# A one-core encoder layer: the places of TensorE's two operands modulo 512 bytes are changed by pads

## The chip, the core and the metric

The kernel runs on one core of one Trainium2 chip. The metric is the device time of one execution in microseconds (us). The kernel before took 1360.14 us, the median of three runs (1357.89 to 1361.29). About 0.3% of that, 4.1 us, is what a measurement of this kernel can tell from no change.

## What is computed

The program is one layer (depth 1) of a hybrid encoder, in fp32, for a prompt of 1,024 rows and a sample of 64 rows that continues a cache of 512. The reference, cut to its core:

```python
z = einsum('btd,de->bte', x, w_in)               # one projection, split into q, k, v of FoX, gate, SGU u and v, q, k, v of stick-breaking
o_f = softmax(q_f k_f / 8 + c_t - c_s) v_f       # 6 heads x 64, causal, c = cumsum(log_sigmoid gate)
o_s = stick_breaking(q_s k_s / 8) v_s            # 6 heads x 64, strictly causal
o_g = gelu(u) * (tril(w_s) layer_norm(gelu(v)) + b_s)
mix = (per_head_rms_norm([o_f, o_g, o_s]) * g_mix) @ w_out
x1  = layer_norm(2**0.25 * x + mix)
y   = layer_norm(2**0.25 * x1 + square(relu(x1 @ w_up)) @ w_down)
```

The outputs are y and the new rows of k, v, the log gate and the normalised v.

## The kernel before, in words

**Operands.** Every fp32 operand of a large product is kept as a high and a low part (type fp32r), and a product is three passes: high x high, high x low, low x high. So each product is a train of matmuls that accumulate into one PSUM bank, and each matmul has its own weight load (PEld), which runs while the matmul ahead of it streams. The operand that is loaded is called stationary here (128 columns), the one that streams is called moving (256, 262, 288 or 512 columns).

**Stages, in order of time.** From 0 to about 530 us: projections of keys and values (`tok_mm`, L490, moving `wkvfox`, `wkvsb`, `wu`, `wv`, stationary the transposed input `xT`), projections of queries (L631, moving `xT`, stationary `wqfox`, `wqsb`), and attention: scores (L691), transposes by the identity (L739), products with the values (L749 to L752), the sample's products (L829 to L875). To about 660 us: the output projection `mix` (L373, moving `w_out`, stationary `oTb`). To about 980 us: the up projection (`product`, L1441; stationary `ws`, `wa`, moving `xo`). It works by seven products a block pair over two row groups, `NS = (288, 256)`, so that twelve matmuls of 288 columns and twelve of 256 mostly alternate. To the end: the down projection (`Down.product`, L1906, and the sample's L1950 and L1952; moving `wd`, stationary `h4a`, `h4b`), then the last norm.

The lines of the matmuls say which operand is which, since the call's second argument is stationary and its third is moving:

```python
490   nc.tensor.matmul(acc[0:n, c0:c0 + n1 - n0], xT[k // 4][:, k % 4, c:c + n], wt[:, k, hw, n0:n1],
373   nc.tensor.matmul(acc[0:m], oT[:, k, hx, 0:m], wo[k // 4][hw][:, k % 4, cs],
631   nc.tensor.matmul(acc[:, 0:w], wq[:, k, hw, :], xT[k // 4][:, k % 4, c:c + w],
749   nc.tensor.matmul(o[:, 0:256], v0, pth[:, 0, 0:256], start=(m == 0), stop=False)
1441  nc.tensor.matmul(z, w[:, hw, k], xop(s, bo, hx)[:, k, :], start=(new and k == 0 and j == 0),
1906  nc.tensor.matmul(z, h[:, hx, q, o], wset[self.c % 2][q][:, hw, wb],
```

**Order.** Four tables written out in the kernel (`ORDER`, one for TensorE, ScalarE, VectorE and GpSimd) fix the order of each engine's instructions. They are the same before and after. DMAs go out on SyncE's queue in program order.

**Where tiles lie.** Tiles come from pools. `cp`, `big` (tag `xw`: `xT`, `xo`, and `wd` later) and `sp` grow from the left end of a partition, `sa`, `lp` and `dp` serve the attention and the two MLP halves. A tile's address follows from the tiles that its pool placed earlier, so a small unused tile moves what comes behind it. `pad(pool, n)` (L242) places such a tile of n bytes a partition.

**Place.** In this document the place of a matmul is the start of its moving operand minus the start of its stationary operand, in bytes within a partition, modulo 512. It follows from the addresses that the built program gives its tiles. Both programs have 8,827 matmuls in the same order, as many as the trace has matmul records, so each record has its place. Place 448 means that the moving operand starts 64 bytes below the stationary one.

Of the kernel before, what the change touches and what calls it, by code (L numbers as in the profile page):

```python
# [13 lines left out]
F32 = mybir.dt.float32  # L14
F32R = mybir.dt.float32r
# [6 lines left out]
P = 128  # L22
PASSES = ((0, 0), (0, 1), (1, 0))
D = 1024
# [4 lines left out]
NB = TP // P  # L29
NT = NB + 1  # L30
# [13 lines left out]
ROWS = 7  # L44
# [129 lines left out]
def _build(nc, tc, a, es):  # L174
    def trows(t):
        return P if t < NB else TS

    cp = es.enter_context(tc.tile_pool(name="cp", bufs=1, side="left"))
    big = es.enter_context(tc.tile_pool(name="big", bufs=2, side="left"))
# [9 lines left out]
    def flat(n):  # L189
        return a[n].rearrange("l b t h d -> (l b t) (h d)")  # L190
# [7 lines left out]
    ident = cp.tile([P, P], F32, name="ident")  # L198
# [15 lines left out]
    def lo_sub(eng, out, src, hi):  # L214
        eng.tensor_tensor(out, src, hi.bitcast(F32), op=ALU.subtract)  # L215
# [26 lines left out]
    def pad(pool, n):  # L242

        n_pad.append(pool.tile([P, n // 4], F32, name=f"pad{len(n_pad)}", tag=f"pad{len(n_pad)}"))
# [161 lines left out]
    ps = es.enter_context(tc.tile_pool(name="ps", bufs=2, space=PSUM))  # L406
    p12 = ExitStack()
    sp = p12.enter_context(tc.tile_pool(name="sp", bufs=1, side="left"))
    lsum = sp.tile([P, NT, 6], F32, name="lsum")
    nc.gpsimd.memset(lsum, 1.0)  # L410
    gmx = sp.tile([P, KT], F32, name="gmx")
    with ExitStack() as p1:
        sa = p1.enter_context(tc.tile_pool(name="sa", bufs=1, side="right"))
# [4 lines left out]
        def mask(name, base, fill):  # L418
            m = sp.tile([P, P], F32, name=name + "_f", tag="gl", bufs=3)
            nc.gpsimd.memset(m, 0.0)  # L420
            nc.gpsimd.affine_select(m, m, pattern=[[-1, P]], compare_op=ALU.is_ge,
                                    fill=fill, base=base, channel_multiplier=1)
            r = sp.tile([P, P], F32R, name=name)
            nc.vector.tensor_copy(r, m)
            return r

        m_fox = mask("m_fox", 0, BIG)
        m_sb = mask("m_sb", -1, -BIG)

        xT = [big.tile([P, 4, 2 * TT], F32R, name=f"xT{i}", tag="xw") for i in range(2)]  # L430

# [8 lines left out]
        def x_trans(t, xr):  # L440
            n = trows(t)
            for g in range(2):
                pt = ps.tile([P, 4, P], F32, name=f"xtp{t}_{g}", tag=("s", "pt")[g], bufs=2)
                for k in range(4):
                    c = (4 * g + k) * P
                    nc.tensor.transpose(pt[:, k, 0:n], xr[0:n, c:c + P], ident[0:n, 0:n])
                hi = xT[g][:, :, t * P:t * P + n]
                nc.scalar.activation(hi, pt[:, :, 0:n], AF.Copy)
                lc = LO + t * P if t < NB else TT
                lo_sub(nc.vector, xT[g][:, :, lc:lc + n], pt[:, :, 0:n], hi)  # L450
# [30 lines left out]
        def tok_mm(acc, c0, wt, t, n0, n1, ks=range(KT)):  # L481
            seq = []
            for k in ks:
                if t < NB:
                    seq += [(P, k, hx * LO + t * P, hw) for (hx, hw) in PASSES]
                else:
                    two = [(P, k, TP, 0), (TS, k, TP, 1)]
                    seq += two if k == ks[0] else two[::-1]
            for i, (n, k, c, hw) in enumerate(seq):
                nc.tensor.matmul(acc[0:n, c0:c0 + n1 - n0], xT[k // 4][:, k % 4, c:c + n], wt[:, k, hw, n0:n1],  # L490
                                 start=(i == 0), stop=(i == len(seq) - 1))
                if (i + 1) % 8 == 0 and i + 1 < len(seq):
                    yield 0.109 * 8
                    flush()

        def fold(eng, out, acc, c0, n):
            eng.tensor_tensor(out, out, acc[TS:P, c0:c0 + n], op=ALU.add)
# [76 lines left out]
        def k_stack(pk, kpiece, n, nm):  # L574
            for h in range(2):
                nc.scalar.activation(kpiece[0:DH, h, 0:n], pk[h * DH:(h + 1) * DH, 0:n], AF.Copy)
                lo_sub(nc.vector, kpiece[DH:P, h, 0:n], pk[h * DH:(h + 1) * DH, 0:n], kpiece[0:DH, h, 0:n])

        def kv_stage(st, tiles, kpiece, vpiece):
            j, wkv, nv = st["nm"], st["wkv"], st["nv"]  # L580
            kcol = st["hp"] * P
            kvs = []
            for i, t in enumerate(tiles):
                n = trows(t)
                if st["first"]:
                    x_trans(t, xrs[t])
                acc = ps.tile([P, 512], F32, name=f"kv{j}_{t}", tag="acc", bufs=2)
                yield from tok_mm(acc, 0, wkv, t, 0, nv)
                kv = sa.tile([P, 256], F32, name=f"kvs{j}_{t}", tag="kvs", bufs=2)
                kvs.append(kv)  # L590
                nc.scalar.activation(kv[0:n], acc[0:n, 0:256], AF.Copy)
                if nv > 256:
                    nc.vector.tensor_copy(fx[0:n, t, :], acc[0:n, 256:262])
                if t == NB:
                    fold(nc.vector, kv[0:n], acc, 0, 256)
                    if nv > 256:
                        fold(nc.vector, fx[0:n, t, :], acc, 256, 6)
                g = 0 if t < NB else 1
                r0 = t * P if t < NB else 0
                nc.sync.dma_start(flat(st["ok"][g])[r0:r0 + n, kcol:kcol + P], kv[0:n, 0:P])  # L600
                nc.sync.dma_start(flat(st["ov"][g])[r0:r0 + n, kcol:kcol + P], kv[0:n, P:2 * P])
                vs = kv[0:n, P:2 * P].rearrange("p (h c) -> p h c", h=2)
                vh = vpiece[0:n, i, :, 0:DH]
                nc.gpsimd.tensor_copy(vh, vs)
                lo_sub(nc.gpsimd, vpiece[0:n, i, :, DH:P], vs, vh)
                if i + 1 < len(tiles):
                    yield 0.109 * 8

            def finish():
                tot = 0  # L610
                pk = ps.tile([P, 2 * P], F32, name=f"pk{j}_{tiles[0]}", tag="tr", bufs=1)
                for kv, t in zip(kvs, tiles):
                    n = trows(t)
                    nc.tensor.transpose(pk[:, tot:tot + n], kv[0:n, 0:P], ident[0:n, 0:n])
                    tot += n
                k_stack(pk[:, 0:tot], kpiece, tot, f"{j}_{tiles[0]}")

            later.append(finish)
            yield 0.109 * 8
# [387 lines left out]
        for fox, hp in ((True, 2), (True, 1), (True, 0), (False, 0), (False, 1), (False, 2)):  # L1007
            first = not pairs
# [34 lines left out]
        def kv_all(j, us=range(5)):  # L1043
            st = pairs[j]
            nm = st["nm"]
            for u in us:
                if u == 4:
                    if st["first"]:
                        forget(0)
                    yield from slots("kn", 1, 1)  # L1050
                    st["kn"] = sa.tile([P, 2, TS], F32R, name=f"kn{nm}", tag="kn", bufs=1)
                    st["vn"] = sa.tile([P, 1, 2, P], F32R, name=f"vn{nm}", tag="vn", bufs=1)
                    yield from kv_stage(st, [NB], st["kn"], st["vn"])
                    continue
                yield from slots("kp", 1, 8)
                kt = sa.tile([P, 2, 256], F32R, name=f"kp{nm}_{u}", tag="kp", bufs=10)
                if st["first"] and u == 0:
                    pad(sa, 64)
                vt = sa.tile([P, 2, 2, P], F32R, name=f"vp{nm}_{u}", tag="vp", bufs=10)
                st["kp"].append(kt)  # L1060
                st["vp"].append(vt)
                yield from kv_stage(st, [2 * u, 2 * u + 1], kt, vt)
# [3 lines left out]
        def slots(tag, n, cap):  # L1066
            while live[tag] + n > cap:
                yield None
            live[tag] += n
# [225 lines left out]
    xo1 = []  # L1295
# [197 lines left out]
    for i in range(MIXED, NT):  # L1493
        t = ORD[i]
# [13 lines left out]
            back.append(x_samp())  # L1508

    n1 = 4 * 2 * NS[1]  # L1510
    xw = [big.tile([P, 16 + q * n1], F32R, name=f"xo1{q}", tag="xw")[:, 16:] for q in (4, 3)]
    xo1 += [x.rearrange("p (o k h c) -> p o k h c", o=q, k=4, h=2) for x, q in zip(xw, (4, 3))]
    prep0_b(raws0, 1 - ORD.index(ORD[-1]) % 2)
    x2, x3 = x_pair(2), x_pair(3)
# [112 lines left out]
    with p3:  # L1627
# [55 lines left out]
        t = ORD[-1]  # L1683
# [52 lines left out]
        with in_order(border):  # L1736
            ch = chain(1, 0)
            ch.product(0)
            raw = up_load(2)
# [114 lines left out]
    with ExitStack() as p3:  # L1854
        dp = p3.enter_context(tc.tile_pool(name="dp", bufs=1, side="right", reuse_waits="tile"))
# [102 lines left out]
        lst = {}  # L1958

        def norm(t):  # L1960
            if t not in lst:

                lst[t] = ident[:, 16 * t:16 * t + 16] if t < NB else dp.tile([P, 40], F32, name="lstb")
            return lst[t]

        def moments(t, half, n=P):
# [295 lines left out]
    for eng, e in (("PE", nc.tensor), ("ACT", nc.scalar), ("DVE", nc.vector), ("POOL", nc.gpsimd)):  # L2262
        left = [i for i in traced[from_here:] if i.engine == e.engine]
        prev = None
        for word in ORDER[eng].split():
            n, k = (int(x or d) for x, d in zip(re.match(r"(\d*)\+?(\d*)", word).groups(), (1, 0)))
# [30 lines left out]
```

## Time and profile before

| | |
|---|---|
| median of three runs | 1360.14 us |
| the profiled execution's own time | 1360.14 us |
| span of its trace | 1358.4 us |
| mean granted TensorE clock | 0.992 |
| PE (matmul) busy, share of the span | 1305.0 us, 96% |
| PEld (weight load) | 1190.8 us, 88% |
| DVE, ACT, POOL | 73%, 53%, 46% |
| chain that ended last, by engine | PE 71%, DVE 12%, DMA 6%, POOL 4%, ACT 4%, issue 3% |

[...] The pace is the time between the starts of two matmuls, and where a row of the chain of waits holds a train of n matmuls of one kind, its length divided by n is the pace.

### The profile page before, as it was taken

How to read it: one execution, taken by the hardware profiler on the slowest of the kernel's cores; microseconds unless marked ns; L12 is line 12 of the kernel's file. 1: busy time of each engine (PE TensorE's matmuls, PEld its weight loads, DVE VectorE, ACT ScalarE, POOL GpSimd, SP SyncE). 2: the span in 40 equal slices, each digit the busy share in tenths (PEclk: the TensorE clock that was granted, in tenths of full speed). 3: DMA queues.
4: the chain of work that ended last, by engine and by line, in shares of the span. 5: the costliest groups of instructions: out<-in, count | busy, mean ns of one | idle time of the engine just before them, and what ended most of it. 6: DMA issues, size and time to landing. Idle time of an engine off the chain costs nothing.

```text
span 1358.4 us, 24318 instructions
## 1 busy us (share of the span) xinstructions
PE 1305.0 (96%) x8827; PEld 1190.8 (88%) x8827; DVE 998.3 (73%) x1797; ACT 719.3 (53%) x1561; POOL 620.6 (46%) x666
## 2 busy tenths in 40 slices
PE   7999999999988998999999999999999999999996
PEld 7998989999988998778899999999987787887874
DVE  4577666676889289779886777778688677768777
ACT  4366666576656376335523222233267676767765
POOL 3222222255775356766512221212176665665647
PEclk9999999999999999999999999999999999999998
DMA  7435565131312257532234444344568334434333
GB/s 228 111 113 152 150 203 150 52 97 40 91 31 69 65 164 262 155 122 76 79 123 142 156 137 155 122 160 144 180 242 282 124 132 159 138 126 161 121 118 132
DMA packets 158048, 185.64 MB, mean 137 GB/s; under 512 B 27740, under 2 KB 116124, under 8 KB 157928
## 3 DMA queue, kind: packets, MB, share of 16 engines
q1 hardware_dynamic: 155832, 183.01, 42.1%
q8 instruction: 70, 1.15, 0.4%
q10 hardware_dynamic: 2096, 1.07, 0.3%
q14 instruction: 50, 0.41, 0.1%
HBM read 117.65 MB, written 60.10 MB: 131 GB/s over the span
## 4 chain that ended last, share of the span: by engine, by line
PE 71%; DVE 12%; DMA 6%; POOL 4%; ACT 4%; issue 3%; SPq 1%; ACTq 0%; DVEq 0%; POOLq 0%
PE A L1906 10%; PE zA L1441 9%; PE mx L373 6%; PE zD L1441 6%; PE D L1906 5%; PE kvsb L490 5%; PE kvfox L490 3%; PE zB L1441 3%; PE zC L1441 3%; PE B L1906 2%; DMA rwo<-w_out 2%; PE qsb L631 2%; PE Sfox L691 1%; PE qfox L631 1%; DVE snsb L675 1%
## 5 line engine op out<-in xcount | busy, mean ns | idle before, releaser
L215 POOL TENSOR_TENSOR wa<-wr,wa 128x512 fp32r<-128x512 f32 x41 | 62.3, 1546 | 217.9 <-ACT wa L1379 217.9
L215 POOL TENSOR_TENSOR wd<-rd,wd 128x512 fp32r<-128x512 f32 x77 | 101.1, 1324 | 104.2 <-ACT wd L1379 71.4
L373 PE MATMUL mx<-xT,oTb 128*128 128x512 f32 (+1 forms) x416 | 104.0, 401 | 1.8 <-DVE oTb L215 1.3
L1441 PE MATMUL zD<-xo,ws 128*128 128x288 f32 (+1 forms) x720 | 95.9, 287 | 0.2 <-DVE hh L1455 0.2
L1441 PE MATMUL zA<-xo,ws 128*128 128x288 f32 (+1 forms) x720 | 95.7, 287 | 0.0
L373 PEld LDWEIGHTS mx<-xT,oTb 128*128 128x128 f32 (+1 forms) x416 | 75.7, 187 | 20.3 <-DVE oTb L215 2.2
L1441 PEld LDWEIGHTS zD<-xo,ws 128*128 128x128 f32 x720 | 92.2, 188 | 0.5 <-DVE hh L1455 0.5
L490 PE MATMUL kvfox<-wkvfox,xT 128*128 128x256 f32 (+3 forms) x624 | 89.3, 291 | 3.1 <-ACT wkvfox L466 3.0
L1441 PEld LDWEIGHTS zA<-xo,ws 128*128 128x128 f32 x720 | 92.2, 188 | 0.0
L1573 POOL TENSOR_TENSOR rd<-rd 128x512 f32<-128x512 f32 x56 | 79.5, 1420 | 25.9 <-DVE b L215 23.6
L490 PE MATMUL kvsb<-wkvsb,xT 128*128 128x256 f32 (+1 forms) x624 | 88.0, 285 | 0.3 <-ACT wkvsb L466 0.3
L677 POOL TENSOR_TENSOR sgsb<-sgsb,snsb 128x127 f32<-128x127 f32 (+7 forms) x48 | 59.5, 1243 | 57.5 <-DVE snsb L675 50.4
L1379 ACT ACTIVATE wd<-rd 128x512 fp32r<-128x512 f32 x105 | 63.6, 624 | 40.5 <-POOL rd L1573 23.0
L490 PEld LDWEIGHTS kvfox<-wkvfox,xT 128*128 128x128 f32 (+1 forms) x624 | 80.6, 191 | 4.5 <-ACT wkvfox L466 3.4
L1906 PE MATMUL A<-wd,wd 128*128 128x512 f32 x312 | 83.1, 395 | 1.3 <-DVE acc L1873 1.0
L675 DVE TENSOR_TENSOR_SCAN snsb<-snsb,one 128x128 f32<-128x128 f32 (+7 forms) x48 | 72.2, 1508 | 10.7 <-ACT snsb L674 9.3
L490 PEld LDWEIGHTS kvsb<-wkvsb,xT 128*128 128x128 f32 (+1 forms) x624 | 79.0, 186 | 0.7 <-ACT wkvsb L466 0.5
L1906 PEld LDWEIGHTS A<-wd,wd 128*128 128x128 f32 x312 | 58.2, 188 | 16.7 <-DVE acc L1873 2.2
L1452 ACT ACTIVATE sn<-zA 128x256 f32<-128x256 f32 (+1 forms) x80 | 30.9, 389 | 74.4 <-PE zA L1441 65.7
L1906 PE MATMUL A<-wd,h4a 128*128 128x512 f32 x240 | 64.3, 394 | 1.1 <-DVE acc L1873 0.7
L1662 ACT ACTIVATE ws<-wr 128x1024 fp32r<-128x1024 f32 x28 | 29.1, 1055 | 62.3 <-DVE wr L1391 62.3
L1873 DVE TENSOR_TENSOR acc<-acc,A 128x512 f32<-128x512 f32 x73 | 49.1, 679 | 10.9 <-PE A L1906 10.9
(551 smaller groups left out, 3738.6 us busy)
## 6 DMA issues: line engine op xcount, KB each, us to landing
h_dr<-hh SPq DMA_DIRECT2D x30, 512.0 KB, 3.2
rd<-w_down SPq DMA_DIRECT2D x30, 512.0 KB, 4.4
wr<-w_up SPq DMA_DIRECT2D x13, 1024.0 KB, 5.5
hr<-h_dr SPq DMA_DIRECT2D x31, 384.0 KB, 4.3
h_dr<-hh SPq DMA_DIRECT2D x30, 384.0 KB, 3.7
raw<-w_in SPq DMA_DIRECT2D x44, 256.0 KB, 3.3
wo_dr<-swo SPq DMA_DIRECT2D x32, 256.0 KB, 2.2
xT<-wo_dr SPq DMA_DIRECT2D x8, 1024.0 KB, 8.1
```

The costliest lines, as they stand in the source:

```text
L215: eng.tensor_tensor(out, src, hi.bitcast(F32), op=ALU.subtract)
L373: nc.tensor.matmul(acc[0:m], oT[:, k, hx, 0:m], wo[k // 4][hw][:, k % 4, cs], start=(i == 0), stop=(i == len(seq) - 1))
L490: nc.tensor.matmul(acc[0:n, c0:c0 + n1 - n0], xT[k // 4][:, k % 4, c:c + n], wt[:, k, hw, n0:n1], start=(i == 0), stop=(i == len(seq) - 1))
L631: nc.tensor.matmul(acc[:, 0:w], wq[:, k, hw, :], xT[k // 4][:, k % 4, c:c + w], start=(i == 0), stop=(i == len(seq) - 1))
L675: nc.vector.tensor_tensor_scan(g[:, 0:n][:, ::-1], g[:, 0:n][:, ::-1], one.broadcast_to([P, n]), 1.0, op0=ALU.mult, op1=ALU.bypass)
L677: nc.gpsimd.tensor_tensor(s[:, 0:n - 1], s[:, 0:n - 1], g[:, 1:n], op=ALU.mult)
L1379: nc.scalar.activation(hi, raw, AF.Copy)
L1441: nc.tensor.matmul(z, w[:, hw, k], xop(s, bo, hx)[:, k, :], start=(new and k == 0 and j == 0), stop=(k == 3 and j == 2), skip_group_check= ...
L1452: nc.scalar.activation(c, z, AF.Copy)
L1573: eng.tensor_tensor(r[:, o], r[:, x], r[:, y], op=ALU.subtract)
L1873: nc.vector.tensor_tensor(out, out if other is None else other, bank, op=ALU.add)
L1906: nc.tensor.matmul(z, h[:, hx, q, o], wset[self.c % 2][q][:, hw, wb], start=((n in (0, 3) or n == 1 and self.c == 0) and q == 0 and j == 0 ...
```

## The change

It changes where tiles lie, and one place in an engine's order. An unused tile of 32 bytes, three tags (`row`, `wkv`, `raw`) that are placed ahead of their first use, `lsum`, another pad of 32 bytes and the tag `wq` now stand in `sp` behind the two masks. In `sa` a pad of 64 bytes became 192, and one of 384 bytes is new. The moving operand of the up projection's second row group starts 112 elements into its tile and not 16. `lstb`, the last tile ahead of the down projection's, grows by 128 bytes. No instruction is added, removed or given another size, and the number of semaphore waits on each engine is the same.

```diff
-    lsum = sp.tile([P, NT, 6], F32, name="lsum")
-    nc.gpsimd.memset(lsum, 1.0)
     gmx = sp.tile([P, KT], F32, name="gmx")
...
         m_sb = mask("m_sb", -1, -BIG)
+        pad(sp, 32)
+        for tag, n, bufs in (("row", D, ROWS), ("wkv", 4192, 1), ("raw", 512, 2)):
+            sp.tile([P, n], F32, name=f"at_{tag}", tag=tag, bufs=bufs)
+        lsum = sp.tile([P, NT, 6], F32, name="lsum")
+        nc.gpsimd.memset(lsum, 1.0)
+        pad(sp, 32)
+        sp.tile([P, 2048], F32, name="at_wq", tag="wq", bufs=1)
...
                     st["vn"] = sa.tile([P, 1, 2, P], F32R, name=f"vn{nm}", tag="vn", bufs=1)
+                    if st["first"]:
+                        pad(sa, 384)
...
                 if st["first"] and u == 0:
-                    pad(sa, 64)
+                    pad(sa, 192)
...
-    xw = [big.tile([P, 16 + q * n1], F32R, name=f"xo1{q}", tag="xw")[:, 16:] for q in (4, 3)]
+    xw = [big.tile([P, 112 + q * n1], F32R, name=f"xo1{q}", tag="xw")[:, 112:] for q in (4, 3)]
...
-                lst[t] = ident[:, 16 * t:16 * t + 16] if t < NB else dp.tile([P, 40], F32, name="lstb")
+                lst[t] = ident[:, 16 * t:16 * t + 16] if t < NB else dp.tile([P, 72], F32, name="lstb")
```

The places that follow, by the two built programs:

| matmuls | columns | count | place before | place after |
|---|---|---|---|---|
| mix, L373 | 512 | 416 | 384 | 0 |
| down, L1906, L1950, L1952 | 512 | 552 | 128 | 0 |
| the same | 512 | 168 | 384 | 0 |
| the same | 512 | 752 | 0 | 0 |
| key and value projections, L490 | 256 | 1,456 | 64 | 448 |
| the same, with the gate's columns | 262 | 208 | sixteen places in turn | each 384 more |
| query projections, L631 | 256 (384 and 320: 96) | 480 | 192 | 448 |
| scores, L691 | 256 (128: 96) | 384 | 448 | 448 |
| products with the values, L749 to L752 | 256 (128: 96) | 384 | 64 | 448 |
| up, L1441 | 256 | 588 | 64 | 448 |
| up, L1441 | 256 | 672 | 448 | 320 |
| up, L1441 | 256 | 84 | 0 or 448 | the same |
| up, L1441 | 288 | 1,260 of 1,344 | 64, 192, 320, 448 in turn | the same |
| transposes by the identity | up to 128 | 674 | 384 | 0 |
| sample's values, L871, L875 | 256 | 60 | 448 | 64 |

On GpSimd the order differs at the start of the program, before its first work on data (`wkvfox`). `ident` is the identity, `m_fox_f` and `m_sb_f` are the masks as they are made, `fx` and `rge` are small tables. Before:

```order
masks.py:197 MEMSET ident 128x128
L201 MEMSET negh 128x1
L203 MEMSET one 128x1
L410 MEMSET lsum 128x54
masks.py:199 ISA
masks.py:199 AFFINE_SELECT ident<-ident 128x128
L420 MEMSET m_fox_f 128x128
L420 MEMSET m_sb_f 128x128
L503 MEMSET fx 128x54
L287 MEMSET rge 128x144
L421 AFFINE_SELECT m_fox_f<-m_fox_f 128x128
L421 AFFINE_SELECT m_sb_f<-m_sb_f 128x128
```

and after, in the same stretch:

```order
L418 MEMSET m_fox_f 128x128
masks.py:199 ISA
masks.py:199 AFFINE_SELECT ident<-ident 128x128
L418 MEMSET m_sb_f 128x128
L419 AFFINE_SELECT m_fox_f<-m_fox_f 128x128
L431 MEMSET lsum 128x54
L508 MEMSET fx 128x54
L287 MEMSET rge 128x144
L419 AFFINE_SELECT m_sb_f<-m_sb_f 128x128
```

The memset of `lsum` stands behind the first mask and no longer ahead of the identity's second step; nothing else moved on any engine.

## The prediction, made before the changed kernel ran

> **What bounds the kernel now.** I read the busy time by stretch first. Its columns are the stretch, its length, then busy time and count of PE, PEld, DVE, ACT and POOL, the granted clock, DMA share and GB/s.
>
> ```profile
> 11.00:530.00 519.00, 495.51 (x4011) 478.29 (x4011) 359.41 (x776) 311.03 (x784) 217.03 (x310) 0.99 0.41 116
> 1050.00:1290.00 240.00, 240.00 (x1040) 192.53 (x1039) 176.41 (x272) 165.64 (x331) 147.01 (x119) 1.00 0.41 137
> ```
>
> TensorE is busy nearly throughout, at a granted clock of 0.99 and 1.00, so no throttle can explain the paces below. What a faster matmul is worth differs by stage, and the chain of work that ended last says how much. These are its shares by line for the windows 11 to 530, 530 to 660, 1050 to 1290 and 1290 to the end:
>
> ```profile
> by line: PE kvsb L490 12.5%; PE kvfox L490 8.3%; issue 5.5%; DMA rwo<-w_out 5.2%; PE qsb L631 4.5%; PE Sfox L691 3.5%; PE qfox L631 3.4%; DVE snsb L675 3.3%; PE sgu L490 3.1%; PE Ssb L691 2.9%; PE ptfox L739 2.7%; PE ptsb L739 2.7%; POOL sg
> by line: PE mx L373 64.1%; PE op L329 5.8%; DMA uu<-u_dr 2.5%; DVE ss L316 2.4%; issue 2.4%; DMA oo<-o_dr 2.3%; DMA u_dr<-sguu 2.2%; DVE g1u L889 2.1%; SPq L360 1.9%; DVE oTb L215 1.5%; ACT sq L314 1.4%; DVE pthsb L215 1.1%; PE xtb L1315 0.
> by line: PE A L1906 50.9%; PE D L1906 25.9%; PE B L1906 13.3%; PE ds L1952 5.0%; PE ds L1950 5.0%
> by line: PE A L1906 16.4%; DVE acc L2018 7.1%; POOL awa L2008 6.9%; DVE acc L1916 5.7%; issue 5.3%; DVE acc L2016 4.5%; PE D L1906 4.0%; DVE wd L1605 3.6%; POOL acc L2008 3.5%; POOL acc L2004 3.4%; POOL awa L2004 3.4%; POOL ident L1976 3.2%
> ```
>
> The third row is TensorE alone: from 1050 to 1290 us every nanosecond of pace counts. In the attention the chain runs through DMAs, VectorE and issue too, so part of a gain there is lost.
>
> **Step 1: products of 512 columns go to place 0.** Before, both kinds exist side by side. Rows of the chain of waits (start, length, train of matmuls); the first four trains are wholly at place 0, the next three at 128, the last at 384:
>
> ```profile
> 1105.43 2.50 PE A L1906 x11
> 1110.71 2.73 PE A L1906 x12
> 1185.28 2.51 PE D L1906 x11
> 1198.11 2.75 PE A L1906 x12
> ...
> 1073.92 2.79 PE A L1906 x12
> 1227.42 2.56 PE D L1906 x11
> 1238.79 4.20 PE A L1906 x18
> ...
> 580.47 11.15 PE mx L373 x48
> ```
>
> At place 0: 10.49 us over 46 matmuls, 228.0 ns each. At the other two: 20.70 us over 89, 232.6 ns. The three L1906 trains and the four have the same line, the same operand types and neighbours in time, so the place is what sets them apart: 4.6 ns. It is paid where the chain runs through such matmuls. Mix: 64.1% of 130 us is 83.3 us, or 358 matmuls at 232.6, worth 1.6 us. Down, 1050 to 1290: by places and start times 529 of its matmuls are not at 0, all on the chain, worth 2.4 us. After 1290: 20.4% of 68.4 us is 14.0 us, 60 matmuls, 0.3 us. The 41 of the same lines between 980 and 1050, 0.2 us at most, I leave out. **Sum: 4.3 us.** No engine behind it is near: in the stretch from 1050 DVE is busy 176 of 240 us.
>
> [...]
>
> **Step 2: products of 256 columns.** Here the trace shows two paces for the same work. In order: a train of up projections at place 448, a later one at 448, one at 64, then key projections at 64, two trains of query projections at 192, and last two trains at 448 that follow each other behind a train of 288 columns:
>
> ```profile
> 700.18 1.36 PE zA L1441 x12
> ...
> 936.98 1.41 PE zA L1441 x12
> ...
> 962.17 1.36 PE zD L1441 x12
> ...
> 460.56 4.36 PE kvsb L490 x37
> ...
> 287.09 1.89 PE qsb L631 x16
> 351.67 1.60 PE qsb L631 x14
> ...
> 978.75 1.38 PE zA L1441 x12
> 980.12 1.37 PE zB L1441 x12
> ```
>
> 1.36 us over 12 is 113.3 ns, 1.41 is 117.5. A train keeps its pace; it is no accident of one matmul. Both occur at both places, so the place does not fix the pace; it seems to decide into which pace a disturbance throws the stream. At place 64 the key projections, which are interrupted every few matmuls, run at 117.8 (4.36 us over 37), and no row of theirs with eleven or more is faster than 117. At 448 a stream can recover: the last two rows start with a few slow matmuls and come to 1.38 and 1.37. Of the 23 trains at place 448 with no 288-column train just before, from the one at 697 to the one at 987 us, about 14 are fast; the row at 936.98 is one of the slow. I take a fast share of 0.6 for L490 after the change; with no train of L490 at 448 to look at, this is the weakest number here. L490: 4.5 ns x 1,456 x 0.6 = 3.9 us. On the chain: 12.5, 8.3 and 3.1% of 519 us are 124 us; `sgv`, below the printed shares, may add up to 14; all L490 is about 1,664 x 118 = 196 us, so about 0.7 counts: **2.8 us**. The 384 products with the values go the same way: 4.5 x 384 x 0.6, with half on the chain (an estimate from the stage, as none of their rows is large), **0.5 us**. Ends for both: nothing gained; or all fast, 5.5 us in sum; or worse than now at the dearest 256-column pace, which the next rows give as 119.2: 1.4 ns more, a loss of 1.7 us in sum.
>
> Queries (L631) go from 192, where the two rows show 118.1 and 114.3, to 448: taken at nothing, since both paces exist at both places; from their mean of 116.2, all fast would be 480 x 2.9 and all slow 480 x 1.9 ns; with half on the chain (7.9% of 519 us, 41 us, of the 70 or so that they take) -0.7 and +0.5 us.
>
> Up (L1441), 588 from 64 to 448 and 672 from 448 to 320. Alternating with 288 columns the rows of 24 are, at 64 and then at 448, with a bare train of 288 last:
>
> ```profile
> 709.98 3.00 PE zB L1441 x24
> 712.98 2.94 PE zA L1441 x24
> ...
> 727.86 3.02 PE zA L1441 x24
> 730.88 2.96 PE zB L1441 x24
> ...
> 969.20 1.59 PE zB L1441 x12
> ```
>
> Less the 1.59 us, the 256-column half takes 1.35 to 1.43 us (119.2 ns at most). Means at the two places are 2.97 and 2.99: no gain from 64 to 448 here, where the 288-column train before sets the pace. Place 320 is not shown for 256 columns; it lies between 192 and 448, which both hold the fast pace. I take zero; all fast or all slow is 0.04 us in each of 105 pairs of trains, 4.2 us either way.
>
> **Step 3: the rest, at nothing.** Transposes go from 384 to 0. Groups by form (count, busy us, mean ns) at 384 and 192:
>
> ```profile
> L739 PE MATMUL ptfox<-ident,Tfox 128*128 128x128 f32 x216 | 36.0, 276 | 1.7 <-DVE pthfox L215 1.2 <-ACT Tfox L666 0.5
> L770 PE MATMUL otpfox<-ident,osbfox 128*128 128x128 f32 x48 | 9.2, 272 | 0.0
> ```
>
> Two places, 4 ns apart: at most 674 x 4 x 0.5 = 1.3 us either way. The 262-column matmuls run through sixteen places before and after. The sample's 60 values go back to 64: 0.3 us at worst. The memset that moves on GpSimd:
>
> ```profile
> 1.00 0.15 POOL L410 MEMSET lsum<- 128x54 f32 x1
> 6.28 1.26 POOL L215 TENSOR_TENSOR wkvfox<-raw,wkvfox 128x512 fp32r<-128x512 f32 x1 [3.78 <-ACT wkvfox L466]
> ```
>
> GpSimd then idles 3.78 us for the first weights, which hides it; without that cover it would cost 0.15 us. It issues no DMA.
>
> **The sum.** The profiled execution took 1360.14 us itself, which is also the median (its span is 1358.4). 1360.1 - 4.3 - 2.8 - 0.5 = **1352.5 us**.
>
> **Rivals.**
> - *Only 512 columns gain.* The pace of a 256-column stream comes from what ran before it, not from its place; for it, the slow trains at 448 (936.98). Time 1355.8. Chance 0.2.
> - *Everything goes fast*, the up projection and the queries with it: against it, the alternation with 288 columns, which the change leaves. 4.3 + 5.5 + 0.7 + 4.2 = 14.7, so 1345.4; a partial form about 1347. Chance 0.1.
> - *No effect.* Place is not the cause, but something that goes along with it, such as which buffer holds the operands; then 1360.1. Against it: trains of one line, close in time, at 232.6 and at 228.0. [...] Chance 0.1.
> - *Slower.* Place 320 and 448 hold the slow pace in the mixed streams: the up projection loses its fast halves (+4.2), the queries theirs (+0.5), keys and values go to 119.2 (1.7), transposes lose 1.3. That is 7.7 against 4.3: 1363.5. It decides from the point where the 256-column work loses over 4.3 us, which needs all up trains slow and something more; for it, 672 matmuls leave a place with known fast trains for one not seen. Chance 0.08.
> - My forecast: 0.52, with its own range 1349 to 1355.5.
>
> **Range and chances.** 1346 reaches into the all-fast case, 1358.5 covers the 512-only case and leaves out no effect and slower: 1346 to 1358.5. A change under 0.3% (4.1 us) can't be told from none. Faster by more means below 1356.0: forecast 0.52, all-fast 0.1, somewhat over half of the 512-only case 0.12, in sum 0.74. Within: 0.08 + 0.09 + 0.02 = 0.19. Slower by more: 0.07.
>
> **What would show it.** Right: L1906 and L373 trains at 228 ns everywhere (2.73 to 2.75 us for 12), the window from 530 to 660 shorter in its L373 rows, and L490 rows where 1.36 per 12 stands beside 1.41. Wrong: L373 still at 232; L490 trains at 117.7 throughout (the 512-only case); rows of 24 of the up projection all at 3.02 (the slower case); or a chain in the attention that gives the saved time back to DMA and VectorE waits.

## The result, and the profile after

The changed kernel took 1356.57 us, the median of 16 runs (1353.01 to 1360.89), and the kernel before 1360.14 us in 16 runs beside them. The ratio is 0.9975, 95% interval 0.9963 to 0.9986: faster by 0.25%, 3.4 us. The forecast was 7.6 us. The profiled execution after took 1356.3 us itself, with a span of 1354.6.

The busy time of the two stretches that the prediction began with, after (stretch, its length, then busy time and count of PE, PEld, DVE, ACT and POOL, the granted clock, DMA share and GB/s):

```profile
11.00:530.00 519.00, 493.96 (x4020) 476.81 (x4019) 360.01 (x778) 311.96 (x784) 217.88 (x311) 0.99 0.41 116
1050.00:1290.00 240.00, 239.75 (x1050) 193.68 (x1050) 177.65 (x272) 165.71 (x331) 146.24 (x118) 1.00 0.40 137
```

From 1050 to 1290 us TensorE does ten matmuls more than before (1,050 for 1,040), and for the first time it isn't busy throughout: 239.75 of 240.00. The chain that ended last, by line, in that stretch, after:

```profile
by line: DMA rd<-w_down 18.7%; POOL wd L215 15.7%; POOL rd L1580 13.7%; DMA awa<-h_dr 9.9%; issue 9.5%; ACT wd L1386 7.2%; ACT st L1611 4.7%; ACT wd L1607 2.5%; ACT h4a L1607 2.3%; DVE h4a L1612 2.0%; DVE wd L215 2.0%; POOL hs L215 1.7%; DV
```

Before, this row held nothing but PE L1906, L1950 and L1952. Now no matmul is in it. What bounds the stretch is the **feed** of the down projection: loads of `w_down` (`rd`) and of the hidden rows (`awa`, `h_dr` in DRAM), their splits into high and low parts on ScalarE, GpSimd and VectorE (`wd`), and the sums of weight blocks on GpSimd (`wd_sum`, L1580, L1573 before).

The paces did change. Chain rows after (start, length, train): mix, key projections fast and slow, up at place 320, and rows of 24 with 288 columns, the first with its 256-column products at 448, the second at 320:

```profile
579.22 10.93 PE mx L373 x48
...
453.11 3.76 PE kvsb L495 x33
...
459.79 4.36 PE kvsb L495 x37
...
697.09 1.41 PE zB L1448 x12
...
711.54 2.95 PE zA L1448 x24
...
729.28 3.01 PE zB L1448 x24
```

Mix runs at 227.7 ns (232.3 in its row before). Key projections have trains at 113.9 now beside trains at 117.8; before there was no such row. The up projection's rows of 24 stand at 2.95 or at 3.01, whole blocks of rows long. Each record has its place, so the trace gives the mean time between starts by kind (stops left out; the share is that of gaps up to 115 ns):

| matmuls | before: place, mean ns (share) | after: place, mean ns (share) |
|---|---|---|
| mix, 512 columns | 384: 232.7 | 0: 228.5 |
| down, L1906, 512 columns | 128: 233.0; 384: 233.1; 0: 228.4 | 0: 227.4 |
| key and value projections | 64: 117.7 (0.03) | 448: 116.0 (0.42) |
| query projections | 192: 115.5 (0.51) | 448: 115.4 (0.53) |
| scores | 448: 117.0 (0.23) | 448: 117.8 (0.13) |
| up, the 588 | 64: 116.1 (0.40) | 448: 114.3 (0.80) |
| up, the 672 | 448: 115.5 (0.52) | 320: 117.5 (0.10) |

The sample's 128 products of 512 columns (L1950 and L1952, which alternate) have no part in the gain: their mean was 231.0 ns at place 0 and 232.4 at 384 before, and is 231.2 after.

The starts also split the time of each stage (cut at the same matmuls in both traces, near the borders of the stages) into pace and stops; a stop is what a gap between two starts has beyond the usual pace of its size. In us:

| stage | length before | change | of it pace | of it stops |
|---|---|---|---|---|
| attention | 520.2 | -0.92 | -1.99 | +1.07 |
| mix | 151.7 | -0.95 | -1.33 | +0.38 |
| up | 333.3 | +0.02 | -0.12 | +0.13 |
| down, first 240 matmuls | 61.4 | -0.23 | -0.62 | +0.39 |
| down, next 1,000 | 230.7 | -2.00 | -3.19 | +1.19 |
| the rest | 45.8 | +0.11 | -0.59 | +0.70 |
| sum | 1343.1 | -3.97 | -7.84 | +3.86 |

So the matmuls gained 7.8 us, and half of it was given back in stops. The question is where these come from.

**One stop, read in both traces.** The largest stop of these 1,000 matmuls after is at 1201 us. Rows of the timeline after (start, length, engine; in brackets how long the engine had waited, and for what):

```profile
1195.21 0.63 ACT L1607 ACTIVATE h4b<-awa 128x512 fp32r<-128x512 f32 x1 [1.08 <-DMA awa<-h_dr]
...
1198.00 1.30 POOL L1580 TENSOR_TENSOR rd<-rd 128x512 f32<-128x512 f32 x1 [8.37 <-DVE b L215]
...
1199.33 0.63 ACT L1386 ACTIVATE wd<-rd 128x512 fp32r<-128x512 f32 x1 [0.38 <-POOL rd L1580]
...
1200.69 0.39 PE L1913 MATMUL D<-wd,h4a 128*128 128x512 f32 x1
1200.70 0.58 ACT L1930 ACTIVATE p<-A 128x512 f32<-128x512 f32 x1
...
1201.33 0.50 PE L1913 MATMUL A<-wd,h4a 128*128 128x512 f32 x1 [0.25 <-ACT p L1930]
```

ScalarE keeps the order of its table, in which the copy of `p` stands behind these rows. It waited 1.08 us for hidden rows, GpSimd's sum waited for what followed from that, and ScalarE waited again, 0.38 us, for the sum. So it copied `p` out of PSUM from 1200.70 to 1201.28, and TensorE, which needs that bank for `A`, stood still for 0.25 us and began at 1201.33. The same rows before:

```profile
1197.49 0.63 ACT L1600 ACTIVATE h4b<-awa 128x512 fp32r<-128x512 f32 x1 [1.34 <-DMA awa<-h_dr]
...
1202.98 0.58 ACT L1923 ACTIVATE p<-A 128x512 f32<-128x512 f32 x1
...
1205.00 0.39 PE L1906 MATMUL D<-wd,h4a 128*128 128x512 f32 x1
1205.22 1.07 PE L1906 MATMUL A<-wd,h4a 128*128 128x512 f32 x4
```

The copy ended at 1203.56, 1.7 us ahead of the matmul at 1205.22 that needs it. That was all the slack there was. In the trace after TensorE was here 4.3 us earlier, the hidden rows and the copy only 2.28 us earlier, and the slack was gone. The feed had not become slower: counted from the first of the 1,000 matmuls, all 21 copies `p<-A` of the stretch begin between 0.44 us earlier and 0.14 later than before, while TensorE had got 2.3 us ahead when the first stop came.

### The profile page after: what moved, and what is told of

It reads as the page before. It is cut to its first block, busy times and chain, and to the rows that moved or that the text cites. A ratio compares the mean times of both kernels' runs of the same rounds, so it can differ in the third digit from the quotient of the medians.

```text
span 1354.6 us, 24318 instructions
## 1 busy us (share of the span) xinstructions
PE 1297.1 (96%) x8827; PEld 1186.1 (88%) x8827; DVE 998.8 (74%) x1797; ACT 720.1 (53%) x1561; POOL 619.8 (46%) x666
## 3 DMA queue, kind: packets, MB, share of 16 engines
q10 hardware_dynamic: 2096, 1.07, 0.3%
## 4 chain that ended last, share of the span: by engine, by line
PE 50%; DVE 14%; DMA 12%; POOL 10%; ACT 8%; issue 6%; SPq 1%; ACTq 0%; DVEq 0%; POOLq 0%
PE zA L1448 9%; PE zD L1448 6%; PE mx L373 6%; PE kvsb L495 5%; POOL wd L215 4%; DMA rd<-w_down 3%; PE kvfox L495 3%; PE zB L1448 3%; PE zC L1448 3%; POOL rd L1580 3%; DMA rwo<-w_out 2%; DMA awa<-h_dr 2%; DVE snsb L680 2%; ACT wd L1386 1%; PE qfox L636 1%
## 5 line engine op out<-in xcount | busy, mean ns | idle before, releaser
L373 PE MATMUL mx<-xT,oTb 128*128 128x512 f32 (+1 forms) x416 | 102.6, 398 | 1.7 <-DVE oTb L215 1.3
L373 PEld LDWEIGHTS mx<-xT,oTb 128*128 128x128 f32 (+1 forms) x416 | 75.4, 187 | 19.2 <-DVE oTb L215 2.2
L1580 POOL TENSOR_TENSOR rd<-rd 128x512 f32<-128x512 f32 x56 | 79.2, 1415 | 24.5 <-DVE b L215 22.2
L1913 PEld LDWEIGHTS A<-wd,h4a 128*128 128x128 f32 x240 | 44.8, 188 | 12.1 <-ACT wd L1386 1.1
```

Of the source, the lines that this page charges most:

```text
L1580: eng.tensor_tensor(r[:, o], r[:, x], r[:, y], op=ALU.subtract)
```

## The experiments

The theory was from here on: *the feed bounds the down projection as soon as its products go faster, so their gain is lost; relieve the feed, and the gain arrives*. Its rivals: the gain in the down projection isn't there at all; or the stops are an accident of one execution; or VectorE, ScalarE or the loads are the limit, whatever is done to GpSimd.

### One part at a time

The down projection alone, on the kernel before:

```diff
-dp.tile([P, 40], F32, name="lstb")
+dp.tile([P, 72], F32, name="lstb")
```

> The kernel before with the last edit alone: lstb grows by 128 bytes, so that the 720 down products at places 128 and 384 go to 0 and nothing else moves. Theory A (place sets the pace, and part of it is then lost to a feed of weights that is nearly late): all L1906 trains at 227 to 228 ns, 720 x 5.4 = 3.9 us of pace, of which 2 to 2.5 us arrive at the end, ratio about 0.998, with some short stops of PE between 1050 and 1290 us that before has not. Rival B (the pace gain arrives whole and the loss lies in the attention): ratio 0.997, no stops. Rival C (the buffer and not the place): pace stays at 232 to 233, ratio 1.000.

Measured: 0.9991 (0.9979 to 1.0002). Its L1906 products run at 227.3 ns, a pace gain of 3.1 us in the 1,000 matmuls; stops there give back 1.89 and the first 240 another 1.24. Alone, the part that the forecast valued at 2.7 us is not told apart from nothing; the interval reaches from a loss of 0.3 us to a gain of 2.9.

Attention and mix alone, the change with these two undone:

```diff
-dp.tile([P, 72], F32, name="lstb")
+dp.tile([P, 40], F32, name="lstb")
-big.tile([P, 112 + q * n1], F32R, name=f"xo1{q}", tag="xw")[:, 112:]
+big.tile([P, 16 + q * n1], F32R, name=f"xo1{q}", tag="xw")[:, 16:]
```

> The change without its edits of the up and down projections: the pads of the attention alone, so that L373 goes from 384 to 0, and L490 and the products with the values from 64 to 448. Theory A: L373 at 228.5 ns (1.7 us of pace), L490 from 117.7 to about 116 with nearly half its matmuls at 113 to 114 (2.5 us of pace); under half of this arrives, since the attention's chain runs through DMAs and VectorE: ratio 0.9985 to 0.9995. Rival B: the attention is paid as far as TensorE is on the chain, 0.7: ratio about 0.9975.

Measured: 0.9993 (0.998 to 1.0006). Mix at 228.5 ns, key projections at 116.0 with a fast share of 0.43. With the old products the down projection has no stop, and its chain is TensorE alone again:

```profile
by line: PE A L1913 51.4%; PE D L1913 26.1%; PE B L1913 13.3%; PE ds L1959 4.6%; PE ds L1957 4.6%
```

The trace has the gain (attention -2.49 us, mix -1.09), the measured ratio doesn't show it clearly; the interval holds both nothing and 2.7 us. It doesn't hold the forecast for these two stages, 4.9 us.

### The up projection's places

The change, with the second row group's operand started elsewhere (16, 80 or 0 elements in, for 112):

```diff
-    xw = [big.tile([P, 112 + q * n1], F32R, name=f"xo1{q}", tag="xw")[:, 112:] for q in (4, 3)]
+    xw = [big.tile([P, 80 + q * n1], F32R, name=f"xo1{q}", tag="xw")[:, 80:] for q in (4, 3)]
```

> The change without its edit of the up projection (moving operand again 16 elements into its tile): 256-column products at places 64 and 448 and not at 448 and 320. Theory A (320 is a place of the slow pace): the mean 256-column pace of the up projection goes from 116.0 (114.3 at 448, 117.5 at 320) back to 115.8 (116.1 and 115.5), so 0.0 to 0.4 us faster than the change, ratio against before 0.997 to 0.9975. Rival: the edit of the up projection carries a gain that one trace does not show, then this is slower than the change by 1 us or more, ratio 0.9985.

> The change with the up projection's moving operand 80 elements into its tile: 256-column products at 320 (636) and 192 (672). Theory A (each place has its pace): those at 320 stay at about 117.5; those at 192 come to 114 to 115.5, as the query projections at 192 have 55% of theirs at the fast pace; sum about that of the change, within 1 us. Rival (the fast share comes from the 288-column train ahead, not from the place): the halves that ran at 117.5 and 114.3 keep their paces whatever their places, so the first half is at 114 and the second at 117.5.

> The change, with the moving operand of the up projection's second row group at the very start of its tile: 636 of its 256-column products come to place 0 and 672 to place 384. Theory that the place acts modulo 256 (0, and 128 for 384): both halves leave the places 64 and 192 where fast trains exist; the 31 products that stand at 0 and 128 in the trace of after ran at 118.5 to 119.5 ns, so the mean goes from 115.8 to about 119 and the up projection gets about 4 us longer. Rival (the sum of the two halves is the same wherever they lie, as in the runs at 64 and 448, and at 320 and 192): mean 115.8 to 116.1, up projection within 0.4 us of before's 333.3 us.

Measured, the mean of the 588 and of the 672 products, and the stage against before:

| start, elements | places | mean ns | length of the stage | ratio to before |
|---|---|---|---|---|
| 112 (the change) | 448 / 320 | 114.3 / 117.5 | +0.02 us | 0.9975 |
| 16 | 64 / 448 | 116.2 / 115.5 | +0.22 us | 0.9977 (0.996 to 0.9994) |
| 80 | 320 / 192 | 116.3 / 115.5 | +0.16 us | 0.9979 (0.9965 to 0.9993) |
| 0 | 0 / 384 | 119.6 / 119.4 | +4.92 us | one run, 1361.03 us |

Starts of 16 and 80 gave the same paces (116.2 and 116.3, 115.5 and 115.5 ns) although their places are 256 bytes apart: in these runs it was the place modulo 256 that counted. At 0 and 128 of those 256 bytes hardly a matmul was fast (shares 0.00 and 0.08). The rows of the run with the start at 0 show it too: a train of 256 columns at 384, then two rows of 24 with 288 columns and place 0:

```profile
695.11 1.44 PE zB L1448 x12
...
706.77 3.03 PE zB L1448 x24
709.81 3.03 PE zA L1448 x24
```

With the three other starts the sum of the halves stays, so the change of this stage is neutral; with the start at 0 the same stage would have cost all that the change brings. The rival that place means nothing in this stage falls.

### Is it 256 or 512 bytes for 512 columns, and is 64 a bad place?

On the kernel before, 136 or 56 elements in `lstb` for 40: the 720 products that were not at 0 go to 256, or to 64 and 448.

> The kernel before with lstb grown by 384 bytes: the 720 down products that the change moves from 128 and 384 to 0 go to 256, nothing else moves. If the pace goes by the place modulo 512, with 0 alone fast, they run at 232 to 234 ns; if it goes by the place modulo 256 (as the up projection's paces at 64 and 448 against 320 and 192 suggest), at 227 to 228.

> The kernel before with lstb grown by 64 bytes: the same 720 down products go to 64 (552) and 448 (168). No pace of 512 columns at these places is known: if only the equal place is fast, 232 to 234 ns; if the pace follows the distance from 0, between 228 and 233; if 448 has for 512 columns what it has for 256, the 168 are faster than the 552.

Measured, one run each. At 256 they run at 227.3 ns, as at 0; at 64 at 230.5 on the mean and at 448 at 233.4. Two rows of TensorE's timeline with 256 (start, length; all 13 matmuls are at 256), then rows of the chain of the run with 64 and 448:

```profile
1070.09 2.88 PE L1906 MATMUL A<-wd,h4a 128*128 128x512 f32 x12
1072.81 0.39 PE L1906 MATMUL D<-wd,h4a 128*128 128x512 f32 x1
```

```profile
1067.76 4.16 PE A L1906 x18
1071.92 1.40 PE D L1906 x6
1073.32 2.80 PE A L1906 x12
```

From 1070.09 to 1072.81 are 2.72 us over 12 matmuls, 226.7 ns. The three rows of the other run are all at 64: 4.16 over 18 is 231.1, and 2.80 over 12 is 233.3, so at 64 the trains of 512 columns didn't have one pace in this run. With 256 the whole took 1360.19 us: of 2.97 us of pace in the 1,000 matmuls the stops gave back 3.43.

The second run speaks against a part of the theory: its products were no faster (-0.40 us), and there were 2.48 us of stops all the same. The largest of them, 0.68 us at 1260 us, waits for GpSimd's split of weights that were loaded late. Rows of GpSimd, then the piece of the chain between them; the load begins when the first split ends:

```profile
1250.93 1.30 POOL L215 TENSOR_TENSOR wd<-rd,wd 128x512 fp32r<-128x512 f32 x1 [1.07 <-ACT wd L1379]
1258.99 1.29 POOL L215 TENSOR_TENSOR wd<-rd,wd 128x512 fp32r<-128x512 f32 x1 [6.75 <-ACT wd L1379]
```

```profile
1252.26 5.99 DMA rd<-w_down
```

Here the load took 5.99 us, while the median of this run's loads of `w_down` in the stretch is 4.5. TensorE was never more than 0.5 us ahead of before's here, and the copies `p<-A` came up to 4.2 us later than before's. So faster products are one way to use up the slack, and a late feed is another; the feed had little slack before the change.

This leaves a rival that no run tests: `lstb` moves the tiles behind it, and moved tiles could make the feed late by themselves. All seven traces with a larger `lstb` and the sums as they were have stops in the 1,000 matmuls, the two with the old `lstb` (before, and attention and mix alone) have none. In the trace after, the feed kept before's times (above), which speaks against the rival there; for the other six it stays open.

### Relieving the feed, with and without the change

Half of each weight sum is left out (the right 256 of 512 columns, so the output differs), with the change and on the kernel before:

```diff
-        eng.tensor_tensor(r[:, o], r[:, x], r[:, y], op=ALU.subtract)
+        eng.tensor_tensor(r[:, o, 0:256], r[:, x, 0:256], r[:, y, 0:256], op=ALU.subtract)
```

> The change, with the four sums of each group of down weights (wd_sum) done on the left 256 of their 512 columns, so that GpSimd has about 0.7 us less in each of 56 sums; the right halves stay unsummed, so the down products use other numbers there. Theory A (the weights' feed takes back part of the pace gain): the stops of TensorE between 1065 and 1290 us, 1.2 to 3.6 us in the four traces with all down products at place 0, go to under 0.5 us, the stretch is 3.0 us shorter than before's, and the whole is 1 to 2.5 us faster than the change: ratio against before about 0.996. Rival B (the stops come from elsewhere, the hidden rows' loads or ScalarE's queue): stops stay at 1 us or more, ratio 0.9975.

> The kernel before with the same half sums, the control. Theory A: before has no stops in this stretch, its feed is hidden, so the stretch stays at 230.7 us and the whole gains only what the start and the end of the down projection wait for GpSimd: ratio 0.998 to 1.000. Rival: the feed costs before as much, then it gains as the change does, ratio about 0.9985 or lower, with a shorter stretch.

Measured: with the change 0.9937 (0.9921 to 0.9953), without 0.9981 (0.9966 to 0.9996). The ratio of the two is 0.9956, 6.0 us (0.0022 either way, from the two intervals). The 1,000 matmuls got 3.66 us shorter with the change, all of it pace, with no stop; without the change they stayed at 230.73 us to the hundredth. What the control gains all the same lies elsewhere; its first 240 down products took 1.2 us less. The chain with change and half sums from 1065 to 1290 us, its shares and a matmul row:

```profile
by line: PE A L1913 52.1%; PE D L1913 26.5%; PE B L1913 13.3%; PE ds L1959 4.2%; PE ds L1957 4.0%
...
1110.11 4.08 PE A L1913 x18
```

TensorE is alone on it once more, now at 226.7 ns. (From 1050 us on, the row still begins with a load and splits, 2.5% of it `rd<-w_down`.)

### The same without leaving anything out

Whole sums again, but some of GpSimd's go to VectorE: the second of each group of four (14 of 56), then the second and third (28 of 56). Each stands in VectorE's order where GpSimd began it in the trace after. (The first expectation calls the sum "wd less its high part"; it is one block of weights less another.)

```diff
-        eng.tensor_tensor(r[:, o], r[:, x], r[:, y], op=ALU.subtract)
+        over = eng is nc.gpsimd and k in (1,)
+        (nc.vector if over else eng).tensor_tensor(r[:, o], r[:, x], r[:, y], op=ALU.subtract)
```

> The change, with 14 of the 56 sums of the down weights (the second of each group of four, wd less its high part) done by VectorE instead of GpSimd, each put into VectorE's order where GpSimd began it in the trace of after. Nothing is left out. Feed theory (TensorE waits in the down projection because the chain of w_down load, GpSimd and ScalarE splits, GpSimd sums delivers the weights late once the products are faster): the stops of TensorE between 1065 and 1290 us, 1.19 us in the trace of after, fall to under 0.6 us; the stretch 1050 to 1290 is 2.6 to 3.7 us shorter than before's (2.0 after); ratio to before 0.994 to 0.9965. Rival (VectorE, 178 of 240 us busy, is itself near the bound, so work moved to it is late there): stops of 1.2 us or more, ratio 0.9975 or above.

> As the run before, with 28 of the 56 sums (the second and third of each group of four) moved to VectorE. Feed theory: GpSimd is relieved further, stops under 0.6 us, ratio 0.993 to 0.9965, unless VectorE takes over as the bound. Rival (VectorE is near the bound): 28 more operations on it cost more than 14, so stops grow beyond those of the run with 14, and the ratio is higher than that run's, 0.9975 or above.

> The kernel before, without the change, with the same 14 of 56 sums of the down weights on VectorE, at the same places in its order: the control of the run where the change and the moved sums stand together (0.9961). Nothing is left out. Feed theory: before, TensorE was slower than the feed and never stopped in the down projection, so relieving GpSimd brings nothing: no stops between 1065 and 1290 us, that stretch within 0.3 us of before's, ratio 0.998 to 1.002; the change is then worth 0.3 to 0.5% on top of relieved sums. Rival (the moved sums are worth something by themselves, elsewhere in the program): ratio 0.9975 or below, and the change is worth no more beside them than alone, about 0.25% or less.

Measured:

| kernel | ratio to before | the 1,000 matmuls | pace | stops |
|---|---|---|---|---|
| change, 14 sums moved | 0.9961 (0.9948 to 0.9975) | -3.43 us | -3.54 | +0.11 |
| change, 28 sums moved | 0.9964 (0.9951 to 0.9978) | -2.66 us | -3.41 | +0.75 |
| before, 14 sums moved | 0.9991 (0.9977 to 1.0005) | +0.03 us | +0.03 | 0.00 |

The first takes the stops away and has the lowest ratio of the kernels here that compute everything, though its interval overlaps the change's own (0.9963 to 0.9986). Its stop of 1201 us is gone; the same two rows in its timeline are

```profile
1194.93 0.58 ACT L1935 ACTIVATE p<-A 128x512 f32<-128x512 f32 x1
...
1196.21 1.52 PE L1918 MATMUL A<-wd,h4a 128*128 128x512 f32 x6
```

with the copy's end at 1195.51, 0.70 us ahead. The rival is refuted for 14 sums: VectorE had room for them (busy 189.19 of 240 us from 1050 to 1290, with 0.11 us of stops). With 28 some stops come back, 0.75 us of them within 3 us at 1207. That is over the 0.6 us that the feed theory allowed, and the rival's sign of more stops than with 14 came, though not its ratio of 0.9975. There the chain holds no VectorE either, though it is busy 194 of 240 us then:

```profile
1199.12 1.30 POOL wd L215
...
1200.44 5.35 DMA rd<-w_down
...
1206.52 1.29 POOL wd L215
...
1207.86 0.50 PE A L1918
```

```profile
1050.00:1290.00 240.00, 239.85 (x1053) 194.48 (x1052) 193.88 (x298) 165.98 (x331) 116.77 (x94) 1.00 0.42 145
```

It is a load of 5.35 us between two splits, as above. What the further 14 sums cost or bring isn't told apart by these two ratios.

The control without the change gains nothing in the down projection. By the ratios the change is worth 0.9961 / 0.9991 = 0.9970 beside moved sums; with some 0.0019 either way that is not told apart from the 0.9975 alone, nor is the 0.9956 of the half sums quite. So that the gain of the down projection was lost to the feed rests on the traces, where stops and lengths differ by more than they vary, and the times agree with it.

## Why the prediction was wrong, point by point

**The step that failed** is the sentence behind the sum of step 1: "No engine behind it is near: in the stretch from 1050 DVE is busy 176 of 240 us", and with it that all of that stretch's gain counts. For the down projection 2.7 us were forecast (2.4 and 0.3). Idle time didn't keep the engines behind TensorE from being late: after, DVE was busy 177.65 of the 240 us, ACT 165.71 and POOL 146.24, and the chain still ran through their loop of load, split, sum, split, next load. At the matmul read above the slack was 1.7 us, and the trace of before could have shown it. The down projection gained 4.4 us of pace over its three stages. In the six traces with all its products at 0 or 256 and the sums as they were, its length against before's trace came to -2.1, -0.7, 0.0, +2.2, +1.1 and -0.3 us: zero on the mean. In the three relieved ones with the change it was -3.8, -3.4 and -3.2. These lengths hold the first 240 matmuls too, which differ by 1 us and more from run to run. In the 1,000 alone (granted clock 1.00 from 1060 to 1290 us before and, of the six, after, with the down projection alone, at 256 and with the up start at 0), the six changed by -2.00, -1.24, -0.94, +0.83, +0.46 and -0.31 us: 0.5 us gained on the mean, of about 3.0 of pace. The three relieved ones gained 3.66, 3.43 and 2.66, and the three that keep the old products changed by 0.03 at most. Taking away the feed's part gives the lost pace back; that is shown for this stage.

By the measured times a second term was too large: attention and mix together (3.3 and 1.6 us) gave 1.0 us when they were changed alone, and 2.7 at most by the interval. The down projection's part alone gave 1.2 us, and its interval holds the forecast too, so that this part was lost rests on the traces.

**512 columns to place 0: right in kind, and more than forecast.** 4.2 ns in mix and 5.6 in the down projection, for 4.6; those that stood at 0 gained 1.0 as well, when their neighbours came there. In pace: mix 1.3 us for 1.6, the down projection 4.4 for 2.7. The rival "no effect" falls with that. There isn't one pace for 512 columns in these runs: 227.3 ns at 0 and 256, 230.5 at 64, 233.0 at 128.

**Key and value projections: right in kind, too large.** The fast share came to 0.42 and not 0.6, and the mean gain to 1.7 ns a matmul, for 2.7 (4.5 x 0.6). The part on the chain was too small in turn: the attention's pace became 2.0 to 2.3 us shorter, and its length is 516.8 us on the mean of the eight traces with place 448, 518.8 on that of the six without (single traces differ by 1 to 2 us, so this is rough). 2.0 us arrived of that pace, where 3.3 were forecast. The trace after shows 0.9 only.

**Queries and up at nothing: right, with another reason.** Up was taken as hardly dependent on place. It does depend on it: the 588 gained 1.8 ns each (1.1 us), the 672 lost 2.0 (1.3 us). The sum was near zero since one half came to the better and the other to the worse place. So the rival "slower" had the right pace at 320 and the wrong one at 448. The bound of 4.2 us either way was a real one; the start at 0 reached it with +4.9.

**Sum.** The pace terms together were 7.6 forecast and 7.8 measured, but that is luck in part: the terms of the attention were too large and that of the down projection too small. What arrived was 3.4 us by the ratio. By the traces' means it is 2.0 in the attention (3.3 forecast), about 1 in mix (1.6) and nothing in the down projection (2.7). The whole range held it, the likeliest case's own did not. The rival in which only 512 columns gain gave 1355.8 us, close to what came, but for another reason: the key projections did gain, and what is missing is missing behind the 512-column products. The prediction's last words named a chain that gives saved time back as a sign of error, and looked for it in the attention only.

**Left open.** Why a stream of 256 columns at one place has two paces, and why the 588 and the 672 have different shares at the same place (0.80 and 0.52 at 448), wasn't found. Nor was the reason for the stops of the first 240 matmuls and of the tail, 0.4 and 0.7 us in the trace after. The share of fast matmuls at one place isn't fixed from run to run either: the 672 at 448, with nothing of that stage changed, had 0.52 and 115.5 ns in some traces (before, the down projection alone) and 0.40 and 116.0 in others (before with half sums, or with the down products at 256).

## What to carry to other kernels

Before a faster engine is counted in full, look up in that stage how early its inputs are: for a few of its waits, the time between the end of what releases it and its start. Busy shares did not tell that here; a slack of 1.7 us at 1205 us ate up what a busy share of 73% seemed to allow. If the slack is smaller than the gain summed up to that point, relieve the feed in the same step: here 14 sums on another engine took the stops of those 1,000 matmuls from 1.19 us to 0.11.

## What the runs showed of the hardware

In these runs the time between two fp32r matmuls went with the distance of their two operands modulo 256 bytes: for 512 columns 227.3 ns at 0, 230.5 at 64, 233.0 at 128, 233.4 at 192 (448). At 64 whole trains ran at 231.1 and at 233.3. It was the distance and not where one operand starts: in the trace before, the products of L1906 at place 0 have both operands at 192 modulo 512 (228.4 ns) or both at 320 (229.7), and those at 128 and 384 have one at each (233.0 and 233.1); after, both are at 192 in all of them (227.4). For 256 columns there were two paces, 113 to 114 and 117 to 120 ns; at 0 and 128 nearly all matmuls had the slow one (119.6 and 119.4 on the mean).

The records of these matmuls overlap: before, those of L1906 last 392 to 396 ns on the mean in its ten largest groups, and the next matmul starts 228 to 233 ns behind the start of one. So a busy TensorE is not a measure of its pace.

After, most stops between 1050 and 1290 us cost more than the wait: the matmuls that end the ones at 1065.85, 1201.33, 1212.20, 1221.40 and 1222.80 us are followed by the next one after 335 to 339 ns, where 227.4 is the mean: 108 to 112 ns more. Behind the stop that ends at 1218.11 the gap is 233 ns.

In the trace after, the granted clock is 0.50 in three stretches before TensorE's last matmuls, from 188.21, 433.97 and 539.79 us on, each 3.41 us long; in the trace before from 69.96 and 435.19 us on, 3.41 us long, and from 537.59 us on, 6.83 us long. No run shows what sets them off. One of these stretches in the attention, after, between its neighbours:

```profile
430.00:434.00 4.00, 2.44 (x18) 1.80 (x16) 4.00 (x6) 1.67 (x6) 3.16 (x3) 1.00 0.14 33
434.00:437.20 3.20, 2.88 (x13) 2.88 (x14) 2.74 (x8) 2.88 (x7) 1.38 (x2) 0.50 0.53 123
437.40:441.00 3.60, 3.60 (x33) 3.60 (x32) 2.63 (x6) 2.51 (x6) 1.91 (x4) 1.00 0.79 180
```

13 matmuls fall into the 3.2 us at a clock of 0.50, 33 into the 3.6 us behind it, and 18 into the 4.0 us ahead, in which TensorE was busy for 2.44. Where such a stretch falls on products of 256 columns (before, the products with the values from 540.64 to 541.49 us), they start 213 to 214 ns apart, for 113 to 120 at the clock of 1.00. By these paces one stretch of 3.41 us can cost 1.5 to 1.6 us (an estimate); two or three more or fewer of them are in the order of the spread of the runs, 1353.01 to 1360.89 us after.
